# One more staging buffer and half-size pieces where the feed-forward reloads its token sums

## The chip, the cores and the metric

The program runs on 1 core of a Trainium2 chip. The metric is the device time of one execution in microseconds (us). All tensors are float32.

## The reference, cut to what matters

One decoder layer on 2048 tokens of width 1024: a mixer (gated linear attention beside dilated attention), its output projection, and a feed-forward block of width 4096. The change lies in the feed-forward block alone:

```python
h = h + jnp.einsum('bsm,md->bsd', mixed, w_out[l])
nm = rmsnorm(h, mlp_norm_g[l])
a = jnp.square(jax.nn.relu(jnp.einsum('bsd,df->bsf', nm, w_ff1[l])))
h = h + jnp.einsum('bsf,fd->bsd', a, w_ff2[l])
```

## The kernel before

**Products.** The product `nm @ w_ff1` is done with a scheme of the Strassen kind: a 2x2 block product costs seven block products instead of eight, of sums of blocks. The tokens are cut into two halves of 1024; in a half, seven sums of token blocks are needed, numbered j = 1..7 and used in the order 1, 2, 5, 6, 3, 4, 7 (`order`). The 4096 columns of the weights go by in groups of 256 (NP = 16 groups a half, 32 in all); for each group seven sums of weight blocks are made. So `jobs1` has 7 x 32 = 224 products, which this document numbers from 0: products 0 to 111 are of the first token half, 105 to 111 are the last group of that half, and 112 is the first product of the second half. Every 32-bit product is made from three products of split numbers (`mm3`, lines 67 to 69: high by high, low by high, high by low), so one product at `product1` is 12 matmuls of 128x512.

**Token sums.** `norm_to_T` (line 993) normalizes a tile of 128 tokens, transposes it, makes the seven sums and stores them to `hTD` in HBM. `reload(j, half)` (line 1013) brings one sum back, 1 MB, into a staging buffer `rb` (DMA, line 1017, issued from SP), and the function it returns splits it into a high part (ACT, line 345) and a low part (DVE, line 346), which stand in `hb` (two tiles for each j; fourteen in all) for the sixteen groups of that half. In the profile, `hb<-rb` are these splits.

**Weights.** `load_w1` loads a group's weights into one of two `w1raw` buffers; `prep1` splits a weight sum into `w1comb` (ACT line 345, DVE line 346) and forms the next sum in place (DVE, lines 1064 to 1069). `prep1` runs two products ahead. After each product DVE or ACT takes it from PSUM into `acc1` (lines 1099 to 1113); at the end of a group DVE forms seven sums of the result (lines 1112 to 1121), and they are stored to `actD`.

**Beginning.** The output projection goes over sixteen tiles of tokens (loop at line 1129). During its last tiles three of the first half's sums (j = 1, 2, 5) are reloaded through the one `rb` there is. After the loop, the sum for product 3 is reloaded, and then one at a time: the split of one, then the load of the next into the same buffer. A second `rb` comes at product 2, and is used by the second half alone.

**Change of halves.** The tile of `hb` for j is free when product 105, 106, ... has used it for the last time. Before, the split of sum k of the second half stands in the program directly behind product 105 + k, and the load of sum k + 2 behind that, through two `rb` buffers in turn. Product 112 + k is the first to use sum k.

**What sets the order.** The program is written in one order; the framework's planner then places each engine's instructions by a simulated time line: of those that are ready the one that stands earliest in the program goes first. So an instruction's place in the program is its priority. Each engine runs its list in order, and one that waits holds back all behind it. The large tiles (`rb`, `hb`, `w1raw`, `w1comb`, `acc1`, `bb`, `tb`, the output projection's `wo`, `mx`, `mT`) share 25 slots of SBUF under one tag; in the compiled program of before they are handed out in the order in which the program first uses the tiles, each when an older tenant is done.

Of the kernel before, what the change touches and what calls it, by code (L numbers as in the profile page):

```python
# [37 lines left out]
RELOAD = (10, 11, 12)  # L38
# [3 lines left out]
def emit(tc, a, stop=99):  # L42
    nc = tc.nc
    V, A, G, T, SP = nc.vector, nc.scalar, nc.gpsimd, nc.tensor, nc.sync
# [6 lines left out]
    def ps(tag):  # L51
        return psum.tile([128, 512], F32, name="ps_" + tag, tag=tag, bufs=BANKS[tag])

    def slot(name, dt=F32, n=SLOT):

        return up.tile([128, SLOT], dt, name=name, tag="u", bufs=25)[:, :n]

    def view(t, shape):
        n = int(np.prod(shape))
        names = "abcd"[:len(shape)]  # L60
        return t[:, :n].rearrange(f"p ({' '.join(names)}) -> p {' '.join(names)}", **dict(zip(names, shape)))
# [4 lines left out]
    def mm3(out, sh, sl, mh, ml, first, last):  # L66
        T.matmul(out, sh, mh, start=first, stop=False)  # L67
        T.matmul(out, sl, mh, start=False, stop=False)  # L68
        T.matmul(out, sh, ml, start=False, stop=last)  # L69
# [72 lines left out]
    hTD = dram.tile([2, 7, 128, 4, 512], F32, name="hTD")  # L142
# [29 lines left out]
    order = (1, 2, 5, 6, 3, 4, 7)  # L172
# [4 lines left out]
    TF = {j: [slot(f"tb{j}", FR) for _ in range(2)] for j in order}  # L177
# [166 lines left out]
    def split(hi, lo, src):  # L344
        A.activation(hi, src, AF.Copy)  # L345
        V.tensor_tensor(lo, src, hi.bitcast(F32), op=OP.subtract)  # L346
# [90 lines left out]
    def reload(j):  # L437
        t = (xp, bp)[order.index(j) % 2][:, :2048]
        SP.dma_start(t, nTD[j - 1].rearrange("p c s -> p (c s)"))
        return lambda: split(*[v[:, :2048] for v in TF[j]], t)  # L440
# [59 lines left out]
    other, back = second_half(), []  # L500
# [420 lines left out]
    for pr in range(4):  # L921
# [3 lines left out]
        for hh, br in seq:  # L925
# [3 lines left out]
            first = len(units)  # L929
# [61 lines left out]
    rb, TF, TB = [slot("rb")], {}, {}  # L991
# [18 lines left out]

    turns = [0]

    def reload(j, half):

        t = rb[turns[0] % len(rb)][:, :2048]
        turns[0] += 1
        SP.dma_start(t, hTD[half, j - 1].rearrange("p c s -> p (c s)"))

        def rest():
            if j not in TF:  # L1020
                TF[j] = [slot(f"hb{j}", FR) for _ in range(2)]
                TB[j] = [view(v, (4, 512)) for v in TF[j]]
            split(*[v[:, :2048] for v in TF[j]], t)

        return rest

    def mix_T(t):
        u = view(slot("mx"), (2, D))
# [11 lines left out]
    NP = FF // 256  # L1040
    jobs1 = [(g, j) for g in range(2 * NP) for j in order]
# [86 lines left out]
    back = []  # L1128
    for at, t in enumerate(tiles):
        u, m = nxt  # L1130
        if at + 1 < NT:
            nxt = mix_T(tiles[at + 1])
        h = u[:, 1]
        p = [ps("a"), ps("a")]
        parts_ = 2 if at < 2 else 1
        for q in range(parts_):
            for n in range(2):
                cs = slice(n * 512, n * 512 + 512)
                for c in range(q * CH // parts_, (q + 1) * CH // parts_):
                    mm3(p[n], m[:, 0, c], m[:, 1, c], WO[c][:, 0, cs], WO[c][:, 1, cs], c == 0, c == CH - 1)  # L1140
                if q == parts_ - 1:
                    V.tensor_tensor(h[:, cs], p[n], u[:, 1, cs], op=OP.add)
        SP.dma_start(hD[t * 128:t * 128 + 128], h)
        if late is not None:
            norm_to_T(*late)
        if back:
            back.pop()()
        if at in RELOAD:
            back.append(reload(order[at - RELOAD[0]], 0))
        if at == W1AT:  # L1150
            load_w1(0)
        if at == W1AT + 1:
            prep1(0)
            prep1(1)
        late = (h, u[:, 0], t)
# [123 lines left out]
        tk = slice(i * 128, i * 128 + 128)  # L1279
        mm3(p, l[:, 0, c, tk], l[:, 1, c, tk], r[:, 0, c], r[:, 1, c], n % 8 == 0 and c == 0, n % 8 == 7 and c == 1)  # L1280

    back = [*back, reload(order[len(RELOAD)], 0)]
    load_w1(1)
    for at in range(7):
        if at == 2:
            norm_to_T(*late)
            rb.append(slot("rb"))
        if back:
            back.pop(0)()
        if len(TF) < 7 and not back:  # L1290
            back.append(reload(order[len(TF)], 0))
        prep1(at + 2)
        product1(at)
    for at in range(7, len(jobs1)):
        if at in (7 * NP - 9, 7 * NP - 8):
            back.append(reload(order[at - 7 * NP + 9], 1))
        prep1(at + 2)
        product1(at)
        if jobs1[at][0] == NP - 1:
            back.pop(0)()  # L1300
            if at + 2 < 7 * NP:
                back.append(reload(order[at + 2 - 7 * NP + 7], 1))
        if at == len(jobs1) - 6:
            for n in range(2):
                load_b(n)
                load_a(n)
        if at in (len(jobs1) - 4, len(jobs1) - 2):
            n = (at + 4 - len(jobs1)) // 2
            prep_b(n)
            prep_a(n)  # L1310
# [3 lines left out]
    for ph, (j, half) in enumerate(phases):  # L1314
        P = [bank() for _ in range(4)]
        for k in range(8):
            n = 8 * ph + k
            prep_a(n + 2)
            at = k + 8 * (1 - half)
# [72 lines left out]
```

## Time and profile before

| | |
|---|---|
| median of 3 runs | 2400.09 us (2397.44 to 2403.56) |
| profiled execution, its own time | 2398.99 us |
| span of the profile | 2397.2 us |
| mean granted TensorE clock | 0.985 |
| PE / DVE / ACT / POOL busy | 2306.6 / 1561.9 / 1148.0 / 583.3 us |

PE is the matmul engine, PEld its weight loads, DVE the vector engine, ACT the scalar engine, POOL the GpSimd engine; SPq and ACTq are the queues that issue DMAs. A row of a timeline has the start in us, the duration, the engine, the line of the kernel, the operation, out<-in by the program's names with shapes, and in brackets the idle time before it and what ended it. A row of the waits has who waited for whom, the total in us, how many times, and the longest. A row of the windows has the length of the window, then the busy time of each engine (with the instructions counted), the granted clock, the share of the DMA engines and GB/s.

### The profile page before, as it was taken

To read this page: it belongs to the slowest core of one execution; us is meant where nothing else is said; L and a number is where in the kernel's file an instruction comes from. 1 tells how busy PE (TensorE), PEld (TensorE's weight loads), DVE (VectorE), ACT (ScalarE), POOL (GpSimd) and SP (SyncE) were. 2 spreads that over 40 slices of the span, in tenths; PEclk is the share of its full clock that TensorE was granted. 3 is DMA by queue.
4 is the path that set the end of the run, shared out by engine and by line. 5 is a ranking of instruction groups with operands and counts; after the bars stand their busy time and mean duration, and the time that the engine had idled before them with its cause. 6 is when DMAs were issued, how large, how long until landed. Compare 5 with 4: busy or idle time off the path is not lost.

```text
span 2397.2 us, 35124 instructions
## 1 busy us (share of the span) xinstructions
PE 2306.6 (96%) x12648; PEld 1989.9 (83%) x12648; DVE 1561.9 (65%) x2879; ACT 1148.0 (48%) x2181; POOL 583.3 (24%) x551
## 2 busy tenths in 40 slices
PE   6999998999999989999999999999999999999998
PEld 5877898779989988888788887888888888888886
DVE  6878666765667668445677778877773455556555
ACT  5565434533767657223455556555563333224323
POOL 5555435446566665100000000000000100001002
PEclk9999999999999999999999999999999999999999
DMA  6457664757888867468664447544467496457653
GB/s 159 120 164 230 213 189 136 206 166 194 213 193 226 225 174 241 154 201 267 203 206 145 145 149 242 176 162 157 155 203 274 155 315 208 168 170 248 217 167 106
DMA packets 342540, 458.13 MB, mean 191 GB/s; under 512 B 19620, under 2 KB 215733, under 8 KB 336094
## 3 DMA queue, kind: packets, MB, share of 16 engines
q1 hardware_dynamic: 313614, 413.15, 56.0%
q10 hardware_dynamic: 28752, 42.74, 5.2%
q8 instruction: 99, 1.62, 0.3%
q14 instruction: 75, 0.61, 0.1%
HBM read 293.51 MB, written 167.02 MB: 192 GB/s over the span
## 4 chain that ended last, share of the span: by engine, by line
PE 77%; DMA 8%; DVE 7%; issue 3%; ACT 3%; POOL 1%; SPq 1%; ACTq 0%; POOLq 0%; DVEq 0%
PE ps_a L67 8%; PE ps_a L68 8%; PE ps_a L69 8%; PE ps_c L67 7%; PE ps_c L69 7%; PE ps_c L68 7%; PE ps_d L67 4%; PE ps_d L69 4%; PE ps_d L68 4%; PE ps_a L672 4%; PE ps_o L67 3%; PE ps_o L68 3%; PE ps_o L69 3%; PE ps_d L653 2%; DMA cmb<-boD 2%
## 5 line engine op out<-in xcount | busy, mean ns | idle before, releaser
L1226 POOL TENSOR_TENSOR suma<-suma,gs 128x512 f32<-128x512 f32 x16 | 23.3, 1472 | 1152.6 <-ACT scr L1224 1152.5
L346 DVE TENSOR_TENSOR ca<-ra,ca 128x1024 fp32r<-128x1024 f32 x112 | 137.7, 1230 | 164.4 <-ACT ca L345 164.4
L345 ACT ACTIVATE ca<-ra 128x1024 fp32r<-128x1024 f32 x112 | 118.0, 1054 | 225.8 <-PE ps_c L69 185.4
L345 ACT ACTIVATE w1comb<-w1raw 128x512 fp32r<-128x512 f32 x224 | 139.6, 627 | 158.7 <-PE ps_c L69 57.7
L644 ACT ACTIVATE pe<-pe,O 128x256 f32<-128x256 f32 (+1 forms) x384 | 157.6, 454 | 89.1 <-DVE O L643 76.3
L672 PE MATMUL ps_a<-v,pt 128*128 128x65 f32 x1200 | 185.1, 258 | 13.3 <-DVE pt L662 8.5
L672 PEld LDWEIGHTS ps_a<-v,pt 128*128 128x128 f32 x1200 | 180.9, 200 | 16.1 <-DVE pt L662 9.5
L346 DVE TENSOR_TENSOR w1comb<-w1raw,w1comb 128x512 fp32r<-128x512 f32 x224 | 153.6, 689 | 53.4 <-ACT w1comb L345 53.2
L653 PE MATMUL ps_d<-ident,pe 128*128 128x128 f32 x600 | 160.9, 284 | 0.0
L643 DVE CUSTOM_DVE_ANT_0 pe<-ps_c,nb 128x256 f32<-128x256 f32 (+1 forms) x384 | 126.6, 360 | 43.4 <-PE ps_d L653 20.6
L204 DVE TENSOR_TENSOR wcomb<-wraw,wcomb 128x512 fp32r<-128x512 f32 (+2 forms) x84 | 101.2, 1210 | 70.3 <-ACT wcomb L202 68.8
L202 ACT ACTIVATE wcomb<-wraw 128x512 fp32r<-128x512 f32 (+2 forms) x126 | 96.3, 773 | 103.7 <-PE ps_a L69 20.8
L345 ACT ACTIVATE cb<-rb 128x1024 fp32r<-128x1024 f32 x56 | 59.4, 1061 | 158.0 <-PE ps_o L68 108.1
L67 PE MATMUL ps_c<-hb,w1comb 128*128 128x512 f32 x336 | 132.2, 393 | 2.8 <-ACT hb L345 2.8
L68 PE MATMUL ps_c<-hb,w1comb 128*128 128x512 f32 x336 | 132.2, 393 | 1.6 <-DVE w1comb L346 1.6
L69 PE MATMUL ps_c<-hb,w1comb 128*128 128x512 f32 x336 | 131.8, 392 | 0.0
L67 PE MATMUL ps_c<-cb,ca 128*128 128x512 f32 x336 | 130.8, 389 | 0.0
L68 PE MATMUL ps_c<-cb,ca 128*128 128x512 f32 x336 | 130.8, 389 | 0.0
L69 PE MATMUL ps_c<-cb,ca 128*128 128x512 f32 x336 | 130.8, 389 | 0.0
L653 PEld LDWEIGHTS ps_d<-ident,pe 128*128 128x128 f32 x600 | 111.1, 190 | 0.4
L94 POOL TENSOR_TENSOR stats<-stats,mhalf 128x1 f32<-128x1 f32 (+1 forms) x64 | 46.4, 730 | 259.3 <-DVE stats L93 216.1
L346 DVE TENSOR_TENSOR cb<-rb,cb 128x1024 fp32r<-128x1024 f32 x56 | 68.2, 1221 | 62.5 <-ACT cb L345 62.3
(351 smaller groups left out, 7330.2 us busy)
## 6 DMA issues: line engine op xcount, KB each, us to landing
ra<-actD SPq DMA_DIRECT2D x56, 1024.0 KB, 6.8
actD<-acc SPq DMA_DIRECT2D x192, 256.0 KB, 2.3
rb<-w_ff SPq DMA_DIRECT2D x72, 512.0 KB, 4.8
w1raw<-w_ff SPq DMA_DIRECT2D x32, 1024.0 KB, 7.3
k<-kD SPq DMA_DIRECT2D x32, 512.0 KB, 11.5
rb<-hTD SPq DMA_DIRECT2D x14, 1024.0 KB, 5.9
wraw<-w_in SPq DMA_DIRECT2D x48, 256.0 KB, 3.4
boD<-O SPq DMA_DIRECT2D x8, 1056.0 KB, 6.2
```

The lines of the kernel that those rows point to most:

```text
L67: T.matmul(out, sh, mh, start=first, stop=False)
L68: T.matmul(out, sl, mh, start=False, stop=False)
L69: T.matmul(out, sh, ml, start=False, stop=last)
L94: G.tensor_tensor(r2, r, mhalf[:, :n], op=OP.pow)
L202: A.activation(hi, src, AF.Copy, scale=sc)
L204: V.tensor_tensor(lo, src, hi.bitcast(F32), op=OP.subtract)
L345: A.activation(hi, src, AF.Copy)
L346: V.tensor_tensor(lo, src, hi.bitcast(F32), op=OP.subtract)
L643: V.tensor_tensor_reduce(p, s, bias, scale=1.0, scalar=BIG, op0=OP.add, op1=OP.min, accum_out=nm)
L644: A.activation(p, p, AF.Exp, bias=nm, scale=-1.0)
L653: T.transpose(pb[:, i * 128:i * 128 + 128], src, ident)
L672: T.matmul(self.b.opsum[:, n % 4], self.pt[:, i * 128:i * 128 + 128], self.b.v[:, blk, cols], start=first, stop=last)
```

## The change

`reload` takes a buffer of its own if one is given. Its second part is a generator: it splits the sum in two pieces of 1024 columns, and stops between them. In the loop of the output projection, and in the first seven products, both pieces are taken at once (`list(...)`).

At the beginning the second `rb` is made ahead of product 0, and the sums for products 3, 4 and 5 are loaded there, one behind the other, into the second `rb`, the first `rb` and a slot of its own (`rt`); the sum for product 6 is loaded at product 1 into the second `rb`, behind the split of the sum for product 3.

At the change of halves the fourteen pieces are spread over products 106 to 116. They stand behind these products: sum 0 both behind 106; sum 1 behind 107 and 108; sum 2 behind 109 and 110; sum 3 behind 110 and 111; sum 4 behind 112 and 113; sum 5 both behind 114; sum 6 behind 115 and 116. The load of sum k + 2 stands behind the second piece of sum k.

```diff
-    def reload(j, half):
-
-        t = rb[turns[0] % len(rb)][:, :2048]
-        turns[0] += 1
-        SP.dma_start(t, hTD[half, j - 1].rearrange("p c s -> p (c s)"))
+    def reload(j, half, t=None):
+
+        if t is None:
+            t = rb[turns[0] % len(rb)]
+            turns[0] += 1
+        SP.dma_start(t[:, :2048], hTD[half, j - 1].rearrange("p c s -> p (c s)"))
 
         def rest():
             if j not in TF:
                 TF[j] = [slot(f"hb{j}", FR) for _ in range(2)]
                 TB[j] = [view(v, (4, 512)) for v in TF[j]]
-            split(*[v[:, :2048] for v in TF[j]], t)
-
-        return rest
+            for cs in (slice(0, 1024), slice(1024, 2048)):
+                split(*[v[:, cs] for v in TF[j]], t[:, cs])
+                yield
+
+        return rest()
...
-            back.pop()()
+            list(back.pop())
...
-    back = [*back, reload(order[len(RELOAD)], 0)]
+    rb.append(slot("rb"))
+    back = [*back, reload(order[3], 0), reload(order[4], 0), reload(order[5], 0, slot("rt"))]
     load_w1(1)
     for at in range(7):
         if at == 2:
             norm_to_T(*late)
-            rb.append(slot("rb"))
         if back:
-            back.pop(0)()
-        if len(TF) < 7 and not back:
-            back.append(reload(order[len(TF)], 0))
+            list(back.pop(0))
+        if at == 1:
+            back.append(reload(order[6], 0))
         prep1(at + 2)
         product1(at)
+
+
+    first, parts_at = 7 * (NP - 1), {}
+    for n in range(14):
+        parts_at.setdefault(first + 1 + n * 4 // 5, []).append(n // 2)
+    halves, begun = {}, set()
     for at in range(7, len(jobs1)):
-        if at in (7 * NP - 9, 7 * NP - 8):
-            back.append(reload(order[at - 7 * NP + 9], 1))
+        if at == first - 2:
+            halves.update({n: reload(order[n], 1) for n in range(2)})
         prep1(at + 2)
         product1(at)
-        if jobs1[at][0] == NP - 1:
-            back.pop(0)()
-            if at + 2 < 7 * NP:
-                back.append(reload(order[at + 2 - 7 * NP + 7], 1))
+        for n in parts_at.get(at, ()):
+            next(halves[n])
+            if n in begun and n + 2 < 7:
+                halves[n + 2] = reload(order[n + 2], 1)
+            begun.add(n)
```

## The prediction

> **What bounds the kernel now.** I read the page first, for the engine that ends last:
>
> ```profile
> span 2397.2 us, 35124 instructions
> PE 2306.6 (96%) x12648; PEld 1989.9 (83%) x12648; DVE 1561.9 (65%) x2879; ACT 1148.0 (48%) x2181; POOL 583.3 (24%) x551
> PE 77%; DMA 8%; DVE 7%; issue 3%; ACT 3%; POOL 1%; SPq 1%; ACTq 0%; POOLq 0%; DVEq 0%
> ```
>
> PE is busy 96% of the span and makes 77% of the chain that ended last, so an edit away from PE counts only where PE stands still for it. Next I read the waits of the two places that the diff touches: the beginning of the feed-forward (1150 to 1215 us) and the change of halves (1452 to 1500 us).
>
> ```profile
> PE ps_c L67 <- ACT hb L345: 2.8, 1, 2.8
> ACT hb L345 <- DMA rb<-hTD: 2.4, 2, 1.2
> ...
> ACT hb L345 <- DMA rb<-hTD: 6.0, 3, 4.5
> PE ps_c L68 <- DVE w1comb L346: 1.6, 1, 1.6
> PE ps_d L67 <- ACT hb L345: 1.3, 1, 1.3
> ```
>
> The reader is to see PE waiting three times: once at the beginning for the high part of a token sum, twice at the change of halves, for a low weight part on DVE and for a high token part on ACT. Third, the timeline of PE at these places:
>
> ```profile
> 1173.80 0.39 PE L67 MATMUL ps_o<-hb,w1comb 128*128 128x512 f32 x1
> ...
> 1180.04 0.39 PE L69 MATMUL ps_a<-hb,w1comb 128*128 128x512 f32 x1
> ...
> 1181.40 0.39 PE L69 MATMUL ps_a<-hb,w1comb 128*128 128x512 f32 x1
> 1184.61 0.79 PE L67 MATMUL ps_c<-hb,w1comb 128*128 128x512 f32 x1 [2.81 <-ACT hb L345]
> ...
> 1190.74 0.42 PE L67 MATMUL ps_a<-hb,w1comb 128*128 128x512 f32 x1
> ...
> 1478.79 0.39 PE L67 MATMUL ps_c<-hb,w1comb 128*128 128x512 f32 x1
> 1480.74 0.51 PE L68 MATMUL ps_c<-hb,w1comb 128*128 128x512 f32 x1 [1.56 <-DVE w1comb L346]
> ...
> 1483.41 0.45 PE L67 MATMUL ps_a<-hb,w1comb 128*128 128x512 f32 x1
> 1485.17 0.50 PE L67 MATMUL ps_d<-hb,w1comb 128*128 128x512 f32 x1 [1.30 <-ACT hb L345]
> ```
>
> From 1180.04 to 1181.40 six matmuls start: 0.2267 us each, so a product of 12 takes 2.72. At the beginning the next one should have started at 1181.63 and started at 1184.61: 2.98 lost. From there to 1190.74 stand 14 matmuls, which took 6.13 instead of 3.17: 2.96 more. **The beginning loses 5.94.** The change of halves loses 1.95 + 1.76 less two paces (0.45) = 3.26; the 11 intervals from 1480.74 to 1483.41 took 2.67 instead of 2.49, 0.18 more: **3.4 in all**. So **9.3 is the ceiling** of what the change can gain by these stalls. Why the 14 were slow, and how full DVE is, the windows tell:
>
> ```profile
> 1185.00:1190.00 5.00, 5.00 (x13) 3.84 (x13) 3.68 (x4) 1.23 (x3) 0.00 (x0) 0.50 0.41 128
> 1480.00:1482.00 2.00, 1.26 (x5) 1.05 (x6) 1.90 (x3) 2.00 (x4) 0.00 (x0) 1.00 0.04 16
> 1156.00:1166.00 10.00, 10.00 (x54) 8.46 (x53) 7.38 (x10) 7.26 (x11) 0.55 (x1) 1.00 0.73 242
> 1166.00:1176.00 10.00, 10.00 (x46) 8.29 (x45) 7.99 (x12) 5.34 (x7) 0.00 (x0) 1.00 0.92 295
> 1436.00:1455.00 19.00, 19.00 (x86) 15.72 (x85) 14.22 (x23) 10.53 (x18) 0.00 (x0) 1.00 0.46 153
> 1475.00:1495.00 20.00, 17.13 (x74) 13.41 (x73) 19.63 (x26) 14.86 (x21) 0.00 (x0) 1.00 0.73 261
> ```
>
> After the idle 2.98 the granted clock is 0.50; behind the idle 1.7 it stayed 1.00. The long stall thus costs double, the short ones do not. The Trainium skill, "TensorE: Matmul & The Clock Gate", section "What's actually happening", has the clock halved after an idle window of about 3.4 us and back after about 3.4 us of work. The trace agrees in kind and differs in size, since 2.98 was enough here and the slow stretch lasted 6.1; by the page's 3.4 the slow matmuls would have cost 1.7, not 2.96, and the sum below would come out 1.3 later.
>
> **The change, part by part.** *Loads at the beginning.* Before, one buffer turns:
>
> ```profile
> DMA to landing us min/median/max: 4.9/5.9/8.9
> w1raw<-w_ff SPq DMA_DIRECT2D x32, 1024.0 KB, 7.3
> ```
> ```profile
> 1146.14 0.39 SPq L1049 DMA_DIRECT2D w1raw<-w_ff  x1
> ...
> 1156.10 0.33 SPq L1017 DMA_DIRECT2D rb<-hTD  x1
> ...
> 1166.60 0.57 SPq L1017 DMA_DIRECT2D rb<-hTD  x1
> ...
> 1176.71 0.33 SPq L1017 DMA_DIRECT2D rb<-hTD  x1
> ```
> ```profile
> 1162.04 1.91 ACT L345 ACTIVATE hb<-rb 128x2048 fp32r<-128x2048 f32 x1
> ...
> 1172.44 1.92 ACT L345 ACTIVATE hb<-rb 128x2048 fp32r<-128x2048 f32 x1 [1.21 <-DMA rb<-hTD]
> ...
> 1182.64 1.91 ACT L345 ACTIVATE hb<-rb 128x2048 fp32r<-128x2048 f32 x1 [1.22 <-DMA rb<-hTD]
> ```
> ```profile
> 1153.79 2.28 DVE L346 TENSOR_TENSOR hb<-rb,hb 128x2048 fp32r<-128x2048 f32 x1
> ...
> 1163.98 2.29 DVE L346 TENSOR_TENSOR hb<-rb,hb 128x2048 fp32r<-128x2048 f32 x1 [1.27 <-ACT hb L345]
> ...
> 1174.39 2.29 DVE L346 TENSOR_TENSOR hb<-rb,hb 128x2048 fp32r<-128x2048 f32 x1 [1.97 <-ACT hb L345]
> ...
> 1184.58 2.29 DVE L346 TENSOR_TENSOR hb<-rb,hb 128x2048 fp32r<-128x2048 f32 x1 [0.99 <-ACT hb L345]
> ```
>
> A load is issued when DVE has made the low part of the one before (1153.79 + 2.28 is 1156.07, the issue 1156.10): 5.8 from issue to the high part (1166.60 to 1172.44), 2 for ACT, 2.3 for DVE, 10.1 to 10.5 a turn, for a product of 2.72. The last sum's high part begins at 1182.64. PE covered part of the delay with two products of group 1 (the banks go round as a, c, d, c, a, d, c, o, so the `ps_o` row at 1173.80 is product 7 and the `ps_a` row at 1180.04 product 8); without them product 6 would have needed its sum at 1181.63 - 2 x 2.72 = 1176.2. With three buffers, load 4 takes the first `rb` where load 3 stood, load 3 the slot that went to `w1raw` at 1146.14, load 5 the next free one; `w1raw` gets its slot about when the first `wo` is done, at the latest by 1153.79, when before DVE wrote into that slot. The landings of these reloads are 4.9 to 8.9 us after the issue, 5.9 in the median; at that all three lie in SBUF by 1160, and the split of sum 4 began at 1162.04 before and need not begin sooner. Load 6 waits for both pieces of sum 3, about 1158; with 5.9 it lands at 1164, with 8.9 (a half more, for the crowd) at 1167, and two pieces more on ACT and DVE (below) are 3.5: 1170.5 against 1176.2. So the DMAs fall off the path, with 5 us to spare. `w1raw` is issued up to 8 us later; product 7, its first user, comes after product 6 now, near 1179, and a median of 7.3 to landing leaves 15. The same seven loads are issued, at 0.33 each on SP; they pass no store that PE waits for. Load 0 of the second half still needs the stores of the last tile.
>
> *DVE at the beginning* is what is late next. In 1156 to 1176 it is busy 7.38 + 7.99, idle 4.63. In that time it now must also make the low part of sum 6 (2.29, from 1184.58) and, as its slot comes later, perhaps all of sum 3 (2.3), and the pieces are dearer:
>
> ```profile
> L345 ACT ACTIVATE cb<-rb 128x1024 fp32r<-128x1024 f32 x56 | 59.4, 1061 | 158.0 <-PE ps_o L68 108.1
> L346 DVE TENSOR_TENSOR cb<-rb,cb 128x1024 fp32r<-128x1024 f32 x56 | 68.2, 1221 | 62.5 <-ACT cb L345 62.3
> ```
>
> The 128x1024 splits take 1.06 and 1.22, so two pieces are 2.44 against 2.29 on DVE and 2.12 against 1.92 on ACT: four sums, 0.6 more on DVE. That is 5.2 into 4.63, and some of the idle time is the norm of the last tile, waiting for its own statistics, and can't be filled. I take 1.5 of stall that stays, in short waits at full clock; ends 0 (the later sums of group 1 give way) and 5.94 (as before). Gain: 5.94 - 1.5 = 4.4.
>
> *Pieces in the projection loop:* three sums, 0.15 on DVE and 0.2 on ACT each, beside PE that is full; counted at nothing, 1 us if that cover is gone.
>
> *Slots:* for a while 26 tiles want 25 slots, until sum 5 is split and `bb`, `tb` of the last norm are free. The late ones are the accumulators of group 1. Nothing in the trace shows that wait; between 0 and one product, 2.7; I take 0, since group 1 moves back behind product 6.
>
> *Change of halves.*
>
> ```profile
> 1472.38 2.29 DVE L346 TENSOR_TENSOR hb<-rb,hb 128x2048 fp32r<-128x2048 f32 x1 [1.31 <-ACT hb L345]
> ...
> 1480.78 2.29 DVE L346 TENSOR_TENSOR hb<-rb,hb 128x2048 fp32r<-128x2048 f32 x1
> ```
>
> In front of the first gap DVE was in a low part for 2.29, with the weight part that PE waited for behind it; in 1475 to 1495 DVE is busy 19.63 of 20, against 14.22 of 19 in the groups before. So DVE is the bound there, and seven sums in pieces add 7 x 0.15 = 1.05 to it. Against that, pieces let a weight part in between, a product starts on its first two chunks with half of a sum (1.0 on ACT and 1.2 on DVE sooner), and the pieces of sums 3 to 6 stand behind the weights of the products ahead of them. But two buffers still turn, load k + 2 waits for both pieces of k, and these stand one to five products later in the program. Ends: all of 3.4 gained, or each of the turns late, below. I take 1.0: both gaps shortened by 1, less the 1.05.
>
> **Sum:** 2398.99 - 4.4 - 1.0 = 2393.6 in terms of the profiled execution. Its time lies 1.1 under the median of the three runs, so 2394.7 in terms of the median; the three spread over 6.1. A change within 0.3% (7.2 us) can't be told from none here.
>
> **The rivals.** *A: both places are cured.* DVE puts group 1's work off and the pieces fit: 2400.1 - 9.3 = 2390.8. For it: only three PE waits of over a microsecond stand in these stretches, and all three hang on the reloads. Against: the 19.63 of 20.
>
> *B: the stall only changes its name.* DVE's 5.2 into 4.63 pushes a weight part instead of the sum, and the change of halves is as before: 2400. A rule that speaks for it is in the Trainium skill, "DMA: Bandwidth & Descriptors", section "Issuing engines are not separate DMA queues": all transfers run on the same 16 engines and interleave, so three at once land later each. The trace agrees that the engines can fill (0.92 in 1166 to 1176); worked out from that row, 295 / 0.92 = 320 GB/s, 3.15 MB need 9.8 us, 1146 to 1156, which is still ahead of 1162.
>
> *C: the turns at the change of halves grow.* The pieces of sums 2, 4 and 6 stand two to five products later, so each turn of their buffer waits d longer in the queue of a full DVE. Three turns make sum 6 late by 3d; once PE idles 3 us the clock halves and 2.96 comes on top. Against the 4.4 of the beginning this loses from 3d = 1.5, and with d = 4 (seven DVE operations of 0.6) it is 12 + 3 - 4.4 = 10 slower, less what products 119 and 120 cover: about 2408. It is past 0.3% from d of about 3. For it: the program order. Against: the loads, 4.9 to 8.9, not the order, were the longer part of a turn, and pieces shorten one by 0.7.
>
> **How the numbers follow.** Forecast 0.37 (its own range 2391 to 2398), A 0.35, B 0.13, C 0.15. Faster by over 0.3% means under 2392.9: A and the lower edge of the forecast, 0.39. Slower is C, 0.15. The rest is within 0.3%, 0.46. The likeliest gives 2394.5. The range goes from A with the scatter of a run, 2388.5, to half of C, 2405.
>
> **What would show it.** Right: no PE wait over 2 us and no clock under 1.00 between 1150 and 1215; load 3 issued near 1146 and load 6 near 1158; products 0 to 6 in order; DVE over 9 of 10 in 1156 to 1176; at the change of halves PE gaps of together 2 to 3. Wrong: a wait for `w1raw` or for a slot near 1160; a window with clock 0.50 behind 1478; PE idle for 3 us or more at a token sum there.

## The result, and the profile after

| | before | after |
|---|---|---|
| median of 20 runs each | 2398.17 us (2392.44 to 2404.43) | 2390.99 us (2385.88 to 2398.50) |
| profiled execution, its own time | 2398.99 us | 2390.69 us |
| span of the profile | 2397.2 us | 2388.9 us |

The ratio of the times is **0.9972, with a 95% interval of 0.9961 to 0.9983**: 7.2 us faster by the medians, between 4.1 and 9.4 by the interval. That is just inside the 0.3% which the prediction called "no change", and it lies between its forecast (2394.5) and its rival A (2390.8). By the time alone it looks like rival A, but part of that is the baseline: the twenty runs of the kernel before have a median 1.9 below that of the three which the prediction started from. By the gain, 7.2 stands midway between the 5.4 of the forecast and the 9.3 of rival A.

For the comparison of the traces I cut the span at the first matmul of a few products (counted as they run on PE, 12 matmuls each):

| stretch | before, us | after, us | difference |
|---|---|---|---|
| start to product 0 | 1158.5 | 1159.6 | +1.1 |
| product 0 to 18 (the beginning) | 56.3 | 50.1 | -6.2 |
| product 18 to 105 | 236.6 | 236.6 | 0.0 |
| product 105 to 128 (change of halves) | 66.3 | 63.3 | -3.0 |
| product 128 to the end | 879.4 | 879.2 | -0.2 |

So the whole difference lies at the two places, and there it is 9.2 beside a ceiling of 9.3 (6.2 where the prediction counted 5.94, and 3.0 where it counted 3.4). The 1.1 at the top arises ahead of the places changed. Product 0 began anywhere between 1153.3 and 1160.4 in the fourteen profiles of this study, so the stages ahead scatter by as much as the change is worth. The pieces in the projection loop, which the prediction counted at nothing, fall into this stretch; what they cost can't be told from its scatter.

The page of the kernel after, its span, its busy times and the chain that ended last, by engine:

```profile
span 2388.9 us, 35162 instructions
PE 2308.0 (97%) x12648; PEld 1992.9 (83%) x12648; DVE 1560.7 (65%) x2893; ACT 1149.4 (48%) x2195; POOL 584.6 (24%) x551
PE 80%; DVE 7%; DMA 6%; issue 2%; ACT 2%; POOL 1%; ACTq 0%; SPq 0%; POOLq 0%; DVEq 0%
```

PE does the same 12648 matmuls, in 2308.0 instead of 2306.6; DVE has 14 instructions more, and its busy time is the same within 1.2. The work did not get less; PE stands still less.

The waits of PE in the two places, kernel after (who waited for whom, total, times, longest):

```profile
PE ps_d L67 <- ACT hb L345: 0.5, 1, 0.5
```

This is the only row, and it belongs to the change of halves. Where the kernel before had a wait of 2.8 at the beginning there is none of PE's in 1150 to 1215. The windows of the kernel after (length, then PE, PEld, DVE, ACT, POOL, clock, DMA share, GB/s); the last row is the one for the change of halves:

```profile
1156.00:1166.00 10.00, 10.00 (x55) 8.44 (x53) 7.71 (x11) 7.46 (x13) 0.55 (x1) 1.00 1.05 342
1166.00:1176.00 10.00, 10.00 (x46) 8.32 (x45) 10.00 (x12) 8.26 (x13) 0.00 (x0) 1.00 0.84 272
1176.00:1186.00 10.00, 10.00 (x45) 8.06 (x45) 9.50 (x17) 5.28 (x10) 0.00 (x0) 1.00 0.94 293
1186.00:1196.00 10.00, 10.00 (x46) 8.29 (x45) 9.11 (x15) 6.14 (x11) 0.00 (x0) 1.00 0.79 249
1150.00:1215.00 65.00, 65.00 (x296) 53.82 (x295) 53.88 (x79) 38.67 (x63) 0.69 (x2) 1.00 0.80 266
1470.00:1490.00 20.00, 19.53 (x87) 15.86 (x86) 19.17 (x28) 16.38 (x26) 0.00 (x0) 1.00 0.74 255
```

PE is full and the clock 1.00 from 1150 to 1215. DVE is busy 17.71 of the first 20, and another 18.61 of the next 20.

And the last two of these stretches in the kernel before, around its stall:

```profile
1176.00:1186.00 10.00, 7.12 (x27) 5.24 (x27) 6.58 (x9) 5.82 (x8) 0.00 (x0) 0.90 0.56 177
1186.00:1196.00 10.00, 10.00 (x35) 7.96 (x34) 4.94 (x8) 2.65 (x5) 0.00 (x0) 0.76 0.38 133
```

DVE had 8.48 idle in these 20 us. That is where the work went that no longer fitted in front of product 6.

The loads and the last splits of the kernel after (SP's timeline first, then ACT's, then DVE's):

```profile
1147.25 0.33 SPq L1018 DMA_DIRECT2D rb<-hTD  x1
1148.40 0.37 SPq L1018 DMA_DIRECT2D rt<-hTD  x1
1157.51 0.61 SPq L1052 DMA_DIRECT2D w1raw<-w_ff  x1
1158.43 0.72 SPq L1018 DMA_DIRECT2D rb<-hTD  x1
```
```profile
1170.49 2.00 ACT L345 ACTIVATE hb<-rb 128x1024 fp32r<-128x1024 f32 x2
```
```profile
1173.43 1.22 DVE L346 TENSOR_TENSOR hb<-rb,hb 128x1024 fp32r<-128x1024 f32 x1
1175.17 1.22 DVE L346 TENSOR_TENSOR hb<-rb,hb 128x1024 fp32r<-128x1024 f32 x1
```
```profile
1176.72 0.39 PE L69 MATMUL ps_d<-hb,w1comb 128*128 128x512 f32 x1
1176.95 0.39 PE L67 MATMUL ps_c<-hb,w1comb 128*128 128x512 f32 x1
```

Sum 6 is loaded at 1158.43 (before: 1176.71), split from 1170.49 on (before: 1182.64), and its last low piece ends at 1176.39; product 6 starts in its turn at 1176.95, one pace of 0.23 behind product 5. The split was done 0.56 us ahead of product 6, and 3.0 ahead of the first matmul that reads this last piece (the third `L69` of the product, at 1179.37).

### The profile page after: what moved, and what is told of

It is laid out like the page before. It is cut to its first block, busy times and chain, and to the rows that moved or that the text cites. A ratio compares the mean times of both kernels' runs of the same rounds, so it can differ in the third digit from the quotient of the medians.

```text
span 2388.9 us, 35162 instructions
## 1 busy us (share of the span) xinstructions
PE 2308.0 (97%) x12648; PEld 1992.9 (83%) x12648; DVE 1560.7 (65%) x2893; ACT 1149.4 (48%) x2195; POOL 584.6 (24%) x551
## 4 chain that ended last, share of the span: by engine, by line
PE 80%; DVE 7%; DMA 6%; issue 2%; ACT 2%; POOL 1%; ACTq 0%; SPq 0%; POOLq 0%; DVEq 0%
PE ps_a L67 8%; PE ps_a L68 8%; PE ps_a L69 8%; PE ps_c L67 7%; PE ps_c L69 7%; PE ps_c L68 7%; PE ps_d L67 4%; PE ps_d L68 4%; PE ps_d L69 4%; PE ps_a L672 4%; PE ps_o L67 3%; PE ps_o L68 3%; PE ps_o L69 3%; PE ps_d L653 2%; PE ps_c L631 2%
## 5 line engine op out<-in xcount | busy, mean ns | idle before, releaser
L345 ACT ACTIVATE w1comb<-w1raw 128x512 fp32r<-128x512 f32 x224 | 140.1, 627 | 157.4 <-PE ps_c L69 56.8
L69 PE MATMUL ps_c<-hb,w1comb 128*128 128x512 f32 x336 | 130.8, 389 | 0.0
L69 PE MATMUL ps_c<-cb,ca 128*128 128x512 f32 x336 | 130.8, 389 | 0.0
```

## The experiments

Differences of a few us in the whole time are near the scatter, so each kernel is judged first by its two stretches (product 0 to 18, product 105 to 128). Where nothing in them differs they repeat to 0.8 us: 50.0 to 50.7 at the beginning as after, 63.3 to 64.1 at the change as after. One exception, of 1.6, is told of below. Each stretch is read from one profile of its kernel.

### Each part alone

`e1_begin`: the beginning as after, the change of halves as before.

```diff
-        for n in parts_at.get(at, ()):
-            next(halves[n])
...
+        if jobs1[at][0] == NP - 1:
+            list(back.pop(0))
+            if at + 2 < 7 * NP:
+                back.append(reload(order[at + 2 - 7 * NP + 7], 1, None, 1))
```

> The beginning as in the changed kernel, the change of halves as in the kernel before (whole splits behind products 105 to 111). My theory now: the two parts are two stalls of their own, and each is cured nearly whole. Then product 0 to product 18 takes 50.1 us (before 56.3, after 50.1), product 105 to product 128 takes 66.3 us (before 66.3, after 63.3), and the time is 6.2 below before, about 2392. The recorded forecast would have 51.9 in the first stretch. If the two parts lean on each other (DVE work put off from the beginning, say), the second stretch changes too.

Measured: 50.5 and 66.4. Time 2392.64, ratio to before 0.9985 (0.9975 to 0.9995), 3.6 us faster with bounds of 1.2 and 6.0.

`e2_change`: the beginning as before, the change of halves as after.

```diff
-    rb.append(slot("rb"))
-    back = [*back, reload(order[3], 0), reload(order[4], 0), reload(order[5], 0, slot("rt"))]
+    back = [*back, reload(order[len(RELOAD)], 0, None, 1)]
...
+            rb.append(slot("rb"))
```

> The beginning as in the kernel before (one buffer, whole splits), the change of halves as in the changed kernel. Two stalls of their own: product 0 to product 18 takes 56.3 us, product 105 to product 128 takes 63.3, the time is 3.0 below before, about 2395. The recorded forecast gives a gain of 1.0 there, 65.3 us. Rival C gives a stretch longer than 66.3.

Measured: 54.7 and 63.8. Time 2395.82, ratio 0.9999 (0.9990 to 1.0007).

The stretches answer: the two stalls are two, each cured by its own part, the second not quite whole (PE still waits 0.9 there). In the whole time the second part can't be told from nothing: its 2.5 lies at the edge of an interval that ends at 2.4 faster. The 54.7 is the exception. This kernel's beginning stalled as the one before did (PE waited 2.4 for the high part of a sum), but the clock came back sooner. The windows around that stall, kernel before and then `e2_change`:

```profile
1184.60:1185.60 1.00, 0.99 (x2) 0.83 (x3) 1.00 (x1) 1.00 (x2) 0.00 (x0) 0.50 0.00 0
...
1189.60:1190.60 1.00, 1.00 (x4) 0.81 (x3) 0.00 (x0) 0.00 (x0) 0.00 (x0) 0.50 1.06 442
1190.60:1191.60 1.00, 1.00 (x5) 0.76 (x5) 0.00 (x0) 0.64 (x2) 0.00 (x0) 0.91 0.38 156
```
```profile
1179.80:1180.80 1.00, 0.97 (x2) 0.83 (x3) 0.99 (x1) 1.00 (x2) 0.00 (x0) 0.50 0.00 0
...
1181.80:1182.80 1.00, 1.00 (x4) 0.81 (x3) 1.00 (x3) 0.06 (x1) 0.00 (x0) 0.50 0.00 0
1182.80:1183.80 1.00, 1.00 (x5) 0.83 (x5) 1.00 (x2) 0.57 (x1) 0.00 (x0) 0.96 0.68 123
```

PE works for about 6 us at half clock in the one, for 3 in the other, and the stretch is 1.6 shorter (0.4 of it is the shorter wait). If many executions of the kernel before are of the shorter kind, the change gains nearer 7.6 than 9.2 in them, which fits the 7.2 of the medians. The last section shows from the traces what decides between the two.

### What cures the beginning: buffers or pieces

`e13_early`: the kernel before with the second buffer made ahead of product 0 and used in turn, whole splits, no third buffer.

```diff
-    back = [*back, reload(order[len(RELOAD)], 0)]
+    rb.append(slot("rb"))
+    back = [*back, reload(order[3], 0), reload(order[4], 0)]
...
+        if at in (0, 1):
+            back.append(reload(order[5 + at], 0))
```

> The kernel before, with the second staging buffer made ahead of product 0 and used in turn with the first, and nothing else: whole splits, old places, no third buffer. If a turn of one buffer is the whole cause at the beginning: product 0 to 18 takes 50.0 to 50.5 us. If halves or the third buffer have a part in it: 52 or more. Product 105 to 128 stays at 66.3 to 66.5.

Measured: 50.5 and 66.2; time 2388.58 beside 2395.55 of one run before.

`e3_two`: the kernel after without its third buffer (the same two lines, splits in pieces).

> The changed kernel without the third buffer at the beginning: the second buffer is still there from the start, sum 5 is loaded into it when sum 3 has been split, sum 6 into the first when sum 4 has been split. If it takes three buffers: sum 6 is loaded only near 1171 us, when sum 4's low part is done, its high part begins near 1177 and its low part ends near 1180, against 1176.95 for product 6, so PE loses about 3 us there, and if the idle reaches 2.98 the clock halves too, 5 to 6 in all (product 0 to 18: 53 to 56 us). If the early second buffer and the order of issue were enough, product 0 to 18 stays at 50.1, since two products of group 1 can stand in for 5.4 us.

Measured: 50.0 and 63.3; time 2386.17. My figure for two buffers was a miss: sum 6 was issued at 1163.12, 8.0 behind product 0 (after: 1158.43, which is 1.2 ahead of it). The expected 1171 would be 11.4 behind it on the clock of the kernel after. Sum 4's low part was done 8.0 behind product 0 here, and product 6 started in its turn, 17.3 behind product 0 as in the kernel after.

`e10_pieces`: the kernel before with nothing but the pieces, one buffer at the beginning.

```diff
-            split(*[v[:, :2048] for v in TF[j]], t)
+            for cs in (slice(0, 1024), slice(1024, 2048)):
+                split(*[v[:, cs] for v in TF[j]], t[:, cs])
```

> The kernel before with one edit: each split of a token sum in two halves of 1024 columns. One buffer at the beginning, the old places, no third buffer. If the halves are what cures the change of halves (there the halves at the old places already gave 63.3 us): product 105 to 128 takes 63.3. At the beginning a turn of the one buffer stays load, high part, low part; the high part of the first half is 1 us sooner, but the buffer is free only after the second low part, 0.15 later: sum 6 begins its high part still near 28 us behind product 0, so PE loses 1 to 3 us (product 0 to 18: 52 to 56). If the halves alone were enough there too, 50.1; then the second and third buffer buy nothing.

Measured: 52.4 and 63.3. Time 2390.86 against 2394.59, ratio 0.9982 (0.9973 to 0.9992).

`e5_whole`: the kernel after with whole splits everywhere, each of the second half where its second piece stood.

```diff
-    def reload(j, half, t=None):
+    def reload(j, half, t=None, pieces=1):
...
-            for cs in (slice(0, 1024), slice(1024, 2048)):
+            for cs in [slice(2048 // pieces * q, 2048 // pieces * (q + 1)) for q in range(pieces)]:
...
-            next(halves[n])
+            if n in begun:
+                next(halves[n])
```

> The changed kernel with whole splits in all places: the buffers and the places of the changed kernel, each split of the second half where its second piece stood. If the halves are what counts at the change: product 105 to 128 is 63.8 to 66.3 us, with a wait for the weights' low part near 1476. At the beginning the buffers should count and not the halves: product 0 to 18 stays near 50.1 to 50.5.

Measured: 50.0 and 66.5; time 2393.59.

The four as a table, product 0 to 18, with the moment at which sum 6's high part began, counted from product 0:

| | one buffer | two | three |
|---|---|---|---|
| whole splits | 56.3 (24.1), e2: 54.7 (24.0) | 50.5 (14.1) | 50.0 (11.0) |
| pieces | 52.4 (23.9) | 50.0 (13.0) | 50.1 (10.9) |

Every kernel with two buffers is cured, and the third buffer and the pieces add at most 0.5, which is within the scatter of the stretch. With one buffer the pieces shorten the stall without curing it: sum 6 is no sooner, but product 6 starts on its first half. The windows across the whole stretch, `e13_early` and then `e10_pieces` in its stall:

```profile
1154.30:1204.80 50.50, 50.17 (x228) 41.38 (x226) 44.34 (x64) 32.77 (x53) 0.55 (x1) 1.00 0.75 242
```
```profile
1175.00:1180.00 5.00, 3.92 (x18) 2.91 (x17) 3.39 (x6) 3.58 (x7) 0.00 (x0) 1.00 0.37 149
1180.00:1185.00 5.00, 5.00 (x22) 4.15 (x23) 3.47 (x4) 3.21 (x5) 0.00 (x0) 1.00 0.29 33
```

PE stands still for 1.1 there (and for 0.7 at another place, for a weight's high part), and the clock stays at 1.00; the half clock, which made half of the loss before, is gone with so short a stall.

### What cures the change of halves: places or pieces

`e6_places`: the kernel after, with both pieces of a sum behind products 105 to 111, where the whole splits stood before.

```diff
-        for n in parts_at.get(at, ()):
-            next(halves[n])
...
+        if jobs1[at][0] == NP - 1:
+            list(back.pop(0))
```

> The changed kernel, but at the change of halves both pieces of a sum stand together behind products 105 to 111, as the whole splits did before: the half pieces alone, without the spreading. If the places are what counts: product 105 to 128 stays at 66.3 us or is 1 longer (seven sums of 0.15 more on DVE), with the wait for the weights' low part still there near 1480. If the size is what counts: about 63.3. In between says that each gives a part.

Measured: 50.5 and 63.3; time 2388.52. The size is what counts. More than that: in the traces this kernel has on every engine the very list of instructions that the kernel after has, one by one (12648 on PE, 2893 on DVE, 2195 on ACT, 551 on POOL). The spreading over products 106 to 116, which is most of what the diff says of this place, doesn't reach the chip at all. That the planner gives a split its turn by the moment at which its tile is free and its load landed, whatever these places, is my reading of it; what is shown is that these places, against the old ones, moved nothing.

Then which engine's pieces? `e11_low` has the high part whole on ACT and the low part in pieces on DVE, `e12_high` the other way round (second half only; the first half is as after).

```diff
+                    if cs.start == 0:
+                        A.activation(hi[:, :2048], t[:, :2048], AF.Copy)
+                    V.tensor_tensor(lo[:, cs], t[:, cs], hi[:, cs].bitcast(F32), op=OP.subtract)
```
```diff
+                    A.activation(hi[:, cs], t[:, cs], AF.Copy)
+                    if cs.start:
+                        V.tensor_tensor(lo[:, :2048], t[:, :2048], hi[:, :2048].bitcast(F32), op=OP.subtract)
```

> The changed kernel, but in the second token half the high part of a sum is made whole (one instruction of 2048 columns on ACT) and only the low part in halves on DVE. With whole splits this stretch took 66.5 us, with halves of both 63.3. If the gain comes from DVE's queue (a whole low part of 2.29 us stands in front of the weights' low part that PE waits for): 63.3 to 64, and no wait for the weights' low part. If it comes from the first half of the high part being there 1 us sooner: the wait of the first product of the new half on ACT stays at 1.3, and 64.5 to 66.5.

> The other half of it: in the second token half the high part in halves on ACT, the low part whole on DVE. If DVE's queue is the cause: 65.5 to 66.5, with the wait for the weights' low part back. If the earlier high part is the cause: 63.3 to 64. If each engine's halves cure one of the two waits: about 64.9 here and 64.9 with the low part alone in halves.

Measured, product 105 to 128: **69.9 with the low part alone in pieces, 64.9 with the high part alone in pieces** (whole 66.3 to 66.5, both 63.3); times 2392.47 and 2388.61. So the theory that a whole low part of 2.29 stands in DVE's queue before the weights falls: with the low part in pieces the stretch was worse than with whole splits, and with the low part whole the wait for the weights' low part was gone. The waits of PE, `e11_low` and `e12_high` (there lines 1029 to 1031 are the splits of the second half):

```profile
PE ps_c L67 <- ACT w1comb L345: 2.5, 1, 2.5
PE ps_c L68 <- DVE w1comb L346: 2.0, 1, 2.0
```
```profile
PE ps_d L67 <- ACT hb L1029: 1.4, 1, 1.4
```

Two things that the pieces of the high part do can be seen in ACT's timeline at the first split of the second half, kernel before (product 105 starts at 1451.48), after (1446.38) and `e12_high` (1441.84):

```profile
1454.17 1.92 ACT L345 ACTIVATE hb<-rb 128x2048 fp32r<-128x2048 f32 x1
```
```profile
1447.71 1.07 ACT L345 ACTIVATE hb<-rb 128x1024 fp32r<-128x1024 f32 x1 [0.50 <-PE ps_c L68]
```
```profile
1443.17 1.07 ACT L1029 ACTIVATE hb<-rb 128x1024 fp32r<-128x1024 f32 x1 [0.50 <-PE ps_c L68]
```

The whole split starts 2.69 behind the start of product 105, when the whole product is through with the tile. The first piece starts 1.33 behind it, half a product sooner, released by a matmul in the middle of product 105: half the tile is free by then. And the low part can follow after 1.07 instead of 1.92. What this does to DVE shows in the 27.2 us from product 105 to the first lost microsecond of the kernel before. DVE's waits and the window, kernel before:

```profile
DVE hb L346 <- ACT hb L345: 2.3, 3, 1.3
DVE acc L1111 <- PE ps_a L69: 0.2, 1, 0.2
```
```profile
1451.50:1478.70 27.20, 27.20 (x121) 22.39 (x120) 24.73 (x31) 18.75 (x25) 0.00 (x0) 1.00 0.73 254
```

and the same 27.2 us of the kernel after:

```profile
DVE acc L1114 <- PE ps_a L69: 0.2, 1, 0.2
```
```profile
1446.40:1473.60 27.20, 27.20 (x122) 22.54 (x121) 27.05 (x39) 21.29 (x32) 0.00 (x0) 1.00 0.70 261
```

PE is full in both. Before, DVE stood idle three times, 2.3 in all, with a low part at the head of its list that waited for ACT's whole high part, and all the weights behind it; after, not once. So DVE enters the tight part with 2.3 us more of work done, and PE waits 0.5 instead of losing 3.4. The same row reads 1.8 in `e5_whole` and 1.9 in `e11_low`, which lost their time, and 1.5 in `e12_high`, which lost half of it.

A second queue changed with it, and the runs don't part the two. ACT too stands idle at the head of its list, in a split that waits for the load of its sum: 6.0 in the kernel before (the row stands in the prediction). The same row of the kernel after, of `e12_high` and of `e11_low`, each in the 48 us from product 105 on:

```profile
ACT hb L345 <- DMA rb<-hTD: 2.2, 2, 1.6
```
```profile
ACT hb L1029 <- DMA rb<-hTD: 3.7, 4, 2.1
```
```profile
ACT hb L1030 <- DMA rb<-hTD: 6.8, 3, 4.3
```

In these 48 us both rows go with the stretch, near enough in order:

| | product 105 to 128 | ACT waits for loads | DVE waits for high parts |
|---|---|---|---|
| `e10_pieces` | 63.3 | 2.0 | 0 |
| after | 63.3 | 2.2 | 0 |
| `e2_change` | 63.8 | 3.8 | 0.6 |
| `e9_dve0` | 64.1 | 4.3 | 0.8 |
| `e12_high` | 64.9 | 3.7 | 1.9 |
| before | 66.3 | 6.0 | 2.5 |
| `e5_whole` | 66.5 | 5.7 | 2.4 |
| `e11_low` | 69.9 | 6.8 | 3.4 |

`e1_begin` and `e13_early` read like before, `e3_two` and `e6_places` like after; the kernels with more work on DVE, below, don't fit in. The two rows hang together. The longest of DVE's idle times in the kernel before, 1.31, ended with a split that ACT had begun only when its load landed, after 4.51 idle; and a load is issued when DVE has made the low part of an earlier sum, which frees the buffer. In `e11_low` ACT's wait lies on PE's path itself: a weight's high part stood behind a sum's split that had waited 1.82 for its load and took 1.91, and PE waited 2.5 for it; behind the two stalls of that kernel the clock was at 0.50. So it is shown that the pieces cure this stall, and that a start half a product earlier and shorter idle times on both engines come with them. Which of the queues PE pays for, DVE's, ACT's or the turn of the buffer that links them, stays open.

### How near DVE is to its limit

`e8_dve` makes the low part of each piece of the second half twice, `e14_dve_once` that of each first piece, `e9_dve0` that of each piece of sums 3 to 6 in the first half. The second copy writes the same numbers.

```diff
                 split(*[v[:, cs] for v in TF[j]], t[:, cs])
+                if half == 1:
+                    V.tensor_tensor(TF[j][1][:, cs], t[:, cs], TF[j][0][:, cs].bitcast(F32), op=OP.subtract)
```
```diff
+                if half == 1 and cs.start == 0:
```
```diff
+                if half == 0 and j in order[3:]:
```

> The changed kernel with the low part of each half piece of the second token half made twice (the same subtraction again): 14 times 1.22 = 17.1 us more on DVE at the change of halves. If DVE is the bound there, as the recorded forecast read it (19.63 busy of 20), PE loses nearly all of it: product 105 to 128 takes 63.3 + 12 to 17. If DVE only does ahead of time what isn't due yet, PE loses the part that the work not yet due doesn't take up: DVE had 0.8 idle in 1470 to 1490 and 2.9 in 1490 to 1510, so some 63.3 + 5 to 12. If it has much room, under 65.

> The changed kernel with the low part of each first piece of the second token half made twice: 7 times 1.22 = 8.5 us more on DVE at the change of halves. With 17.1 more it lost 14.1. If DVE were the bound of every microsecond: 63.3 + 8.5 = 71.8. If DVE has room of 3.0 (17.1 less 14.1): 63.3 + 5.5 = 68.8. If part of the 14.1 was the halved clock behind a long idle time, the room is larger, 5 to 6, and it comes to 66 or so.

> The changed kernel with the low part of each half piece of sums 3 to 6 of the first half made twice: 8 times 1.22 = 9.8 us more on DVE at the beginning. If DVE's hours are the bound there (5.2 to be put into 4.63 of idle time, as the recorded forecast has it, of which the forecast let 1.5 remain as a stall): product 0 to 18 takes 50.1 + 5 to 10. If the weights and accumulations can be put off, as the trace of the changed kernel suggests (DVE 10.00, 9.50 and 8.11 in the ten microseconds each behind 1167): the 9.8 go into later idle time, under 52.

Measured: 77.4 at the change of halves with 17.1 more, 75.3 with 8.5 more, and 56.8 at the beginning with 9.8 more (times 2401.24, 2401.50, 2391.95). There is no room of 3 to 6 us at the change: 8.5 more on DVE cost 12.0, more than their own length. The windows, `e14_dve_once`:

```profile
1472.40:1477.40 5.00, 0.17 (x1) 0.00 (x0) 5.00 (x8) 3.53 (x6) 0.00 (x0) 0.96 0.65 221
1477.40:1482.00 4.60, 0.79 (x1) 0.29 (x1) 3.26 (x4) 4.60 (x9) 0.00 (x0) 0.50 0.29 110
1482.00:1483.00 1.00, 0.97 (x2) 0.84 (x3) 0.99 (x1) 1.00 (x2) 0.00 (x0) 0.50 1.67 367
```

Two idle times, 9.6 us with one matmul in each, and the half clock behind them. The first of PE's waits, 4.9, is for a weight's high part on ACT, and ACT had stood idle at the head of its list for a load (its row in the same kernel):

```profile
1473.87 1.06 ACT L345 ACTIVATE hb<-rb 128x1024 fp32r<-128x1024 f32 x1 [3.12 <-DMA rb<-hTD]
```

That load was issued at 1466.61, when DVE had made the second copy of an earlier sum's piece (1465.33 to 1466.55) and so freed the buffer. The price is not proportional: 17.1 cost 14.1 and 8.5 cost 12.0. The planned lists differ, and what each difference gives is not parted here. What holds is that 8.5 us more on DVE turn the change into a loss; in `e14_dve_once` they do so through the turn of a buffer, and not by DVE's own hours alone.

`e9_dve0` doesn't measure DVE's room at the beginning. PE lost its time in one wait, and DVE was not busy in front of it (PE's wait, and then DVE's, in 1150 to 1170; line 378 is the transpose, 101 the norm, 1069 a sum of weights):

```profile
PE ps_c L378 <- DVE mx L101: 3.4, 1, 3.4
```
```profile
DVE w1raw L1069 <- DMA w1raw<-w_ff: 2.8, 1, 2.8
```

DVE stood idle 2.8 at a sum of weights that waited for the late `w1raw`, with the norm of the last tile behind it, and PE's transposes behind the norm. In the kernel after the same wait of DVE is 1.4, it stands behind the norm, and nothing comes of it. So the later `w1raw` is a weak place that the change has made.

## Why the prediction was right, and where it was not

The result, 7.2 us faster, lies in the range, 3.5 below the predicted time; 1.9 of the 3.5 is the median of three runs that it started from, which stood above that of twenty. (Its sum is 2394.7, and 2394.5 below it; no step accounts for the 0.2.) The mechanism, two stalls of PE that hang on the reloads, was right, and so was the ceiling: 9.2 beside 9.3 went. But in the traces it was rival A, both places cured, that came, and not the forecast, which left 3.9 of the stalls standing. The forecast took 5.4, so two of its terms were too small. That the whole time lies nearer to it than the stretches do is luck: the cures were taken too small and the half clock too dear (below), and the two errors pull against each other. Two of its signs came out otherwise: DVE was busy 8.9 of 10 in 1156 to 1176, not over 9, and PE's gaps at the change of halves were 0.5, not 2 to 3.

**The stall left at the beginning (1.5 of 5.94).** The step that failed is "5.2 into 4.63" of idle time on DVE between 1156 and 1176. The figures were near, but the window was closed without reason: DVE did 17.71 of 20 there, and put off the rest behind product 6, where it had stood idle for 8.48 of 20 before, while PE itself stood still or ran at half clock. PE lost nothing by it. Hours of an engine count up to the moment when PE needs the particular result, not up to the end of a window.

**The change of halves (1.0 of 3.4).** Measured 3.0. The step that failed is "the weight part that PE waited for behind" a low part of 2.29, and with it the charge of 1.05 for dearer pieces on a full DVE. Between the low part that began at 1472.38 and that weight part, at 1479.40, stood eight other operations of DVE, so it was not directly behind. DVE's fullness (19.63 of 20) was read in the window in which PE already stood still. In the 27.2 us ahead of it DVE was not full (24.73): 2.3 idle at the head of its list, and ACT idle for loads beside it. The pieces cost DVE their 1.05, and with them those 2.3 went and the first split started half a product earlier. `e12_high` showed that the high part's pieces alone bring half of it (64.9 between 66.5 and 63.3), and `e11_low` that the low part's alone bring nothing. Which queue PE pays for stays open, as said above.

**Rival C, turns that grow.** It fell with its premise: the place in the program was to set the place in DVE's queue, and it set nothing (`e6_places`). Its mechanism is real, as `e14_dve_once` shows; here the turns went the other way, ACT's wait for loads from 6.0 to 2.2. My "these stand one to five products later in the program", which I held against the change, is true of the code and of nothing else.

**Rival B** fell too: no wait on a weight took the place of the wait on the sum. It was not far off: `e9_dve0` shows the way it would have come.

**The loads.** Load 3 at 1147.25 and load 6 at 1158.43 were as foretold (1146 and 1158), and product 6 ran in its order. But sum 6 landed at 1167.71, 9.3 behind its issue, as the 8.9 for a crowd had it (the DMA engines' share in 1156 to 1166 reads 1.05), and its split was done at 1176.39 instead of 1170.5. The Trainium skill, "DMA: Bandwidth & Descriptors", section "Issuing engines are not separate DMA queues", which the prediction cited, has such transfers interleave on the same 16 engines; the trace agrees in kind. The two pieces waited 2.8 for ACT, and then for a DVE that was busy throughout; 3.5 for "two pieces more on ACT and DVE" was a sum of durations in an empty queue. The slack of 5 up to the start of product 6 was in truth 0.56.

**`w1raw`.** "At the latest by 1153.79" was wrong: issued at 1157.51. It had 15 us to spare by the reckoning, and needed them only for product 7; that a sum of weights can stand ahead of the norm on DVE, as in `e9_dve0`, I had not reckoned.

**The third buffer** I priced nowhere by itself; it buys at most 0.5, as the table shows, and 0.5 is within the scatter.

**The clock.** The prediction put 2.96 to the half clock, from one execution. A like stall cost half of that in `e2_change`. The recorded sum takes one draw, and a dear one, for the rule. The estimate of the last section, 1.1 to 1.8 in the mean of many executions, brings the 9.2 of the stretches to 7.3 to 8.1, beside 7.2 measured. The slow stretch, read as 6.1 from the first slow matmul, is 6.83 by the clock itself: it was at 0.50 from 1183.95 on, when PE still stood still.

## What to carry to other kernels

A second buffer ahead of the loop cured the first stall, and splitting a copy in two cured nearly all of the second; the careful spreading of the pieces over products came out as the same lists of instructions. Compare the compiled lists before reasoning about places. When an engine looks full in the window where PE stands still, look for its idle time in the windows before, and for what stood at the head of its list then. Writing a tile in halves lets the first write begin when half of it has been read for the last time, and the first split started half a product sooner here.

## What the runs showed of the hardware

**The granted clock changes on a grid.** Up to the last matmuls of the span, every change of the granted clock in all fourteen traces lies on a grid of 3.41 us that runs through the whole profile; where the grid lies differs from profile to profile. In the kernel before the clock was at 0.50 from 948.43 on and again from 1183.95 on, 69 steps later. So the slow stretches at the two places are whole steps long: 3.41 in `e2_change` and `e9_dve0`, 6.83 in the kernel before, `e8_dve` and `e11_low`, 10.24 in `e14_dve_once`, and 3.41 for the second one of `e8_dve`. The cells of the grid, kernel before, `e2_change`, and one that kept its clock, `e1_begin`:

```profile
1180.54:1183.95 3.41, 1.25 (x6) 0.71 (x4) 2.08 (x3) 2.19 (x3) 0.00 (x0) 1.00 0.20 82
1183.95:1187.36 3.41, 2.75 (x7) 2.18 (x8) 2.78 (x2) 1.65 (x3) 0.00 (x0) 0.50 0.00 0
1187.36:1190.77 3.41, 3.41 (x10) 2.63 (x9) 1.32 (x3) 0.63 (x1) 0.00 (x0) 0.50 0.83 281
```
```profile
1176.06:1179.47 3.41, 1.32 (x6) 0.75 (x4) 2.08 (x3) 2.55 (x3) 0.00 (x0) 1.00 0.20 84
1179.47:1182.88 3.41, 3.05 (x7) 2.47 (x8) 3.07 (x3) 1.49 (x4) 0.00 (x0) 0.50 0.00 0
```
```profile
1474.01:1477.42 3.41, 1.81 (x8) 1.18 (x8) 3.31 (x6) 2.35 (x3) 0.00 (x0) 1.00 0.45 185
```

At these two places the idle time of PE within one cell goes with the clock of the next. Cells at full clock with 2.09 or more idle were followed by 0.50, those with up to 1.56 were not; between these lie one of 1.59 that was (the second time of `e8_dve`, from several short waits) and one of 1.60 that was not (`e1_begin`). Cells at 0.50 with 0.58 or more idle were followed by another, those with up to 0.36 by 1.00. The stall of the kernel before had 2.16 in one cell and 0.66 in the next, so the clock stayed down for two; that of `e2_change` had 2.09 and 0.36, and it came back after one. The clock of `e9_dve0` fell 0.62 behind the end of its idle time, where the next cell began.

So the same stall is dear or cheap by where it falls on the grid, and nothing in the kernel sets that. An estimate from these figures: for a stall of 2.81, over all places on the grid alike, with a limit for the fall between 1.6 and 2.1 and one for the return between 0.37 and 0.58, the half clock costs 1.1 to 1.8 us in the mean; in the profile of the kernel before it cost 2.96.

The Trainium skill, "TensorE: Matmul & The Clock Gate", section "What's actually happening", has the clock halved after at least one idle window of about 3.4 us, and back after at least one busy window of that length. The lengths here, one, two and three times 3.41, agree with that window; the idle time does not, since 2.09 of 3.41 were enough.
